# Attention layer of a two-layer backbone: maxima kept in SBUF, query norms cut into pieces with PSUM operands, rotation sums on VectorE, latent keys finished tile by tile

## The chip, the cores and the metric

The program runs on one core of a Trainium2 chip, with one launch for the whole network. The metric is device time in microseconds (us) of that core. Three unprofiled runs of the kernel before took 1298.45, 1296.28 and 1297.53 us (median 1297.53). One further execution was profiled; all durations below come from it.

The core has five engines with an instruction queue each: TensorE (PE in the profile, with its weight loads as PEld), VectorE (DVE), ScalarE (ACT), GpSimd (POOL) and SyncE (SP), which issues most DMA transfers here. Each queue is executed in its order; between queues there are only semaphores. PSUM is the memory that TensorE writes to, in banks of 2 KB per partition; SBUF is the large on-chip memory.

## What is computed

Layer 0 is a bidirectional gated DeltaNet over 512 latent and 256 context tokens; layer 1 is grouped-query attention with an axial rotary embedding; each stands between an adaptive RMS norm and a gated residual, and a last RMS norm ends the network. The change lies in layer 1, but for the helper of the norms, which both layers call. Cut to layer 1, the reference is:

```python
u_lat = rms_norm(h_lat, norm_g[1]) * (1 + scale) + shift          # 512 x 1024
u_ctx = rms_norm(h_ctx, norm_g[1]) * (1 + scale_c) + shift_c      # 256 x 1024
q, k, v, z = split(u @ att_w_in)        # 8 query heads, 2 key/value heads of 128
q = rms_norm(q, q_norm_g); k = rms_norm(k, k_norm_g)              # per head
q_lat, k_lat = axial_rope(q_lat), axial_rope(k_lat)
s = q_lat @ concat(k_ctx, k_lat).T * 128 ** -0.5                  # 512 x 768, each head
y = (softmax(s) @ concat(v_ctx, v_lat) * silu(z)) @ att_w_out
out = rms_norm(h_lat + gate * y, final_norm_g)
```

## The kernel before

All matrices are float32, and every product is made of three matmuls: each operand is split into a rounded part ("hi") and a remainder ("lo"), and hi·hi, hi·lo and lo·hi are summed in PSUM. ScalarE casts the hi part from PSUM, VectorE subtracts it for the lo part; for weights GpSimd does both (`split_w`, L1209 and L1210; for the output weights L1520 and L1521).

**Normed inputs and keys.** Token tiles 0 and 1 hold the context, 2 to 5 the latents. `norms1` (L1160) makes the scale factors of the layer's norm with `rsqrt` (L163), an integer first guess and three Newton steps on VectorE; with the argument `room` its values lie in a transposition tile in PSUM (of these tiles, tag "tr", there are two). `u_block(k)` (L1169) transposes and scales input block k of eight on TensorE into such a tile (ht), VectorE scales it in place (L1176), ScalarE casts it (L1177) and VectorE subtracts (L1178), giving uL. `kv_block` (L1236) adds block k into the key/value accumulators kv2 to kv5: the loop over k runs u_block(k+1), then kv_block(k) for the four latent tiles. So all four tiles are finished together after k = 7. Between them lie the context's key norm (`kv_norm`, after k = 2), its turned keys (`k_turned`, `k_to_T`) and the tables of the rotation (`rope_by`).

**First queries.** After the loop come, written out by hand: the gate projection `z_main(0)`, the norm of all latent keys at once (squares on ScalarE L1248, `rsqrt` with room, then the split of the values L1252 and L1253), and in turn the four query tiles of pair 0 (`q_main`, 24 matmuls each, L1348, into half a bank of pg), with the rotation of a key tile and of a query tile beside each. `rotated` (L1259) makes, for a query, x·cos on VectorE into SBUF (L1264), two products of the swapped halves with sin (L1267), and the sum of the two on GpSimd (L1268); for a key the factor of the norm is in these products (L1271, L1272) and GpSimd adds likewise (L1273). `to_T` then transposes the sum on TensorE (L1279) and splits it (L1281, L1282). `q_post` (L1353) calls the rotation, then has ScalarE sum the squares (qj, L1357); behind the last tile it calls `rsqrt` for the eight norms of the pair, all of it in SBUF (lines L174, L175, L185 and three times L188 to L190). The norm isn't applied to the query but in the softmax, as a scale per row.

**The loop of attention.** For u = 0 to 35 one pass does: `scores(u)` for head u div 4 and query tile u mod 4 (six matmuls L1389 into s3), its maximum (VectorE L1391, into a spare column of po, the PSUM tile of the values), its product with the norm (nm, VectorE L1394), the exponential (pr, ScalarE L1397), reciprocal of the sum (L1398) and scaling (L1403); the transposition of the probabilities of pass u−2 in two halves (`turn`, TensorE L1414, ScalarE L1416, VectorE L1417); in every even pass `values` (18 matmuls L1426 into po, then ay on VectorE L1428, and the split of yT on ScalarE L1430 and GpSimd L1431). A piece of other matmuls is woven in: of every eight passes (a block) the first two and the last two hold halves of a gate projection (`z_main`, L1371), passes 2 to 5 the four query tiles of the next pair (`q_main`); each tile's `q_post` runs one pass later, and its `to_T` a pass after that. From u = 27 the pieces are parts of the output projection (L1445), whose weights are loaded and split from u = 25 on, with two staging buffers (wf, L1518, pool "wo").

(The norm of the context's keys lies in one of the two transposition tiles as well, between two blocks.) From the latents' key stage to the end of this loop the order on TensorE, VectorE and ScalarE is as the code is written (`manual_schedule`); the order on GpSimd and SP follows from a scheduler's own timeline.

## Time and profile before

| | |
|---|---|
| unprofiled runs | 1298.45, 1296.28, 1297.53 us |
| profiled execution: its time | 1297.93 us |
| its span, first to last instruction | 1296.2 us |
| mean granted TensorE clock | 0.966 |
| layer 1, from its first key matmul | 977.4 us after the span's start, so 319 us |

In the profile's rows, times are us from the span's start. A timeline row gives start, duration, engine, line, operation, output tile <- input tiles with partitions x elements, and a count when equal neighbours are merged; brackets hold the idle time of the engine just before it and what ended it. TensorE's idle time starts at the modelled end of the last matmul. A row of groups gives busy time and mean ns. A row of stages gives its bounds, then busy time and count for each engine, and after POOL the granted TensorE clock, 1.00 being full speed.

### The profile page before, as it was taken

To read this page: it belongs to the slowest core of one execution; us is meant where nothing else is said; L and a number is where in the kernel's file an instruction comes from. 1 tells how busy PE (TensorE), PEld (TensorE's weight loads), DVE (VectorE), ACT (ScalarE), POOL (GpSimd) and SP (SyncE) were. 2 spreads that over 40 slices of the span, in tenths; PEclk is the share of its full clock that TensorE was granted. 3 is DMA by queue.
4 is the path that set the end of the run, shared out by engine and by line. 5 is a ranking of instruction groups with operands and counts; after the bars stand their busy time and mean duration, and the time that the engine had idled before them with its cause. 6 is when DMAs were issued, how large, how long until landed. Compare 5 with 4: busy or idle time off the path is not lost.

```text
span 1296.2 us, 28116 instructions
## 1 busy us (share of the span) xinstructions
PE 1170.6 (90%) x10803; PEld 940.9 (73%) x10803; DVE 822.0 (63%) x1800; ACT 705.3 (54%) x1892; POOL 641.8 (50%) x503
## 2 busy tenths in 40 slices
PE   3999999999789898999999988897999787989996
PEld 1676778888678777887666655685787677878874
DVE  2688566777897466765888884754346456555535
ACT  3344336665476768963898874633332244545621
POOL 0121132169989998302665785675662234331540
PEclk9999999999899988999999999998999988989998
DMA  9366976355545597539799666454642021010233
GB/s 315 130 220 206 327 245 169 113 167 167 151 123 184 154 269 239 180 125 283 235 247 246 166 181 172 152 166 134 186 133 66 1 65 50 17 34 33 66 98 97
DMA packets 165351, 204.56 MB, mean 158 GB/s; under 512 B 13377, under 2 KB 114914, under 8 KB 164322
## 3 DMA queue, kind: packets, MB, share of 16 engines
q1 hardware_dynamic: 146402, 193.33, 49.0%
q10 hardware_dynamic: 18816, 9.44, 2.5%
q8 instruction: 85, 1.39, 0.4%
q14 instruction: 48, 0.39, 0.1%
HBM read 161.96 MB, written 40.67 MB: 156 GB/s over the span
## 4 chain that ended last, share of the span: by engine, by line
PE 54%; DVE 14%; POOL 9%; DMA 9%; ACT 8%; issue 4%; SPq 1%; ACTq 0%; DVEq 0%; POOLq 0%
PE ks L979 6%; PE g_q L335 5%; PE po L1138 5%; PE g_v L335 4%; PE g_z L335 4%; PE pg L1348 3%; PE su L1034 3%; PE po L1426 2%; PE g_k L335 2%; PE pg L1371 2%; PE pr L1004 2%; POOL wol L872 2%; POOL X L677 2%; PE pso L1445 2%; POOL tmp L676 2%
## 5 line engine op out<-in xcount | busy, mean ns | idle before, releaser
L987 POOL TENSOR_TENSOR S<-S,glb 128x512 f32<-128x512 f32 x88 | 90.1, 1047 | 112.5 <-PE ks L979 112.4
L1138 PE MATMUL po<-woh,y 128*128 128x512 f32 x384 | 127.8, 403 | 11.1 <-ACT y L900 8.3
L335 PE MATMUL g_v<-uh,wh 128*128 128x512 f32 (+1 forms) x256 | 91.5, 357 | 15.7 <-DVE sil_v L362 15.7
L872 POOL TENSOR_TENSOR wol<-wo,woh 128x1024 fp32r<-128x1024 f32 x32 | 76.3, 2390 | 52.7 <-ACT woh L871 52.4
L677 POOL TENSOR_TENSOR X<-X,tmp 128x62 f32<-128x62 f32 (+15 forms) x93 | 96.8, 1040 | 6.5
L979 PE MATMUL ks<-S,ckq 128*64 128x256 f32 x768 | 93.5, 385 | 3.4 <-ACT o L984 2.7
L357 DVE SCALAR_TENSOR_TENSOR acc_v<-g_v,cwv,acc_v 128x510 f32<-128x510 f32 (+3 forms) x128 | 74.4, 609 | 34.7 <-ACT acc_v L354 33.2
L335 PE MATMUL g_z<-uh,wh 128*128 128x512 f32 (+1 forms) x256 | 88.9, 347 | 4.6 <-DVE sil_v L362 4.5
L676 POOL TENSOR_TENSOR tmp<-L,X 128x62 f32<-128x62 f32 (+15 forms) x93 | 89.1, 958 | 6.9
L1138 PEld LDWEIGHTS po<-woh,y 128*128 128x128 f32 x384 | 71.6, 191 | 27.7 <-ACT y L900 9.2
L335 PE MATMUL g_v<-ul,wh 128*128 128x512 f32 (+1 forms) x256 | 90.0, 352 | 0.0
L335 PE MATMUL g_v<-uh,wl 128*128 128x512 f32 (+1 forms) x256 | 89.2, 349 | 0.0
L335 PE MATMUL g_z<-ul,wh 128*128 128x512 f32 (+1 forms) x256 | 87.4, 342 | 0.0
L335 PE MATMUL g_z<-uh,wl 128*128 128x512 f32 (+1 forms) x256 | 87.3, 341 | 0.0
L979 PEld LDWEIGHTS ks<-S,ckq 128*64 128x64 f32 x768 | 50.7, 136 | 42.6 <-ACT o L984 11.7
L1138 PE MATMUL po<-wol,y 128*128 128x512 f32 x192 | 77.6, 404 | 4.0 <-POOL wol L872 4.0
L317 POOL TENSOR_TENSOR wl_k<-w_k,wh_k 128x1024 fp32r<-128x1024 f32 x8 | 19.0, 2386 | 101.8 <-ACT wh_k L316 101.8
L335 PEld LDWEIGHTS g_v<-uh,wh 128*128 128x128 f32 x256 | 50.8, 198 | 22.5 <-DVE sil_v L362 16.4
L1397 ACT ACTIVATE pr<-s,nm,sq 128x768 f32<-128x768 f32 x32 | 31.8, 993 | 62.9 <-DVE nm L1394 62.4
L1348 PE MATMUL pg<-wq,uL 128*128 128x256 f32 x384 | 56.0, 293 | 5.0 <-ACT qj L1357 2.6
L1052 DVE TENSOR_TENSOR S<-su,S 128x512 f32<-128x512 f32 x88 | 56.5, 683 | 4.1 <-PE su L1034 2.9
L982 DVE SCALAR_TENSOR_TENSOR r<-ks,negV,cv 128x128 f32<-128x128 f32 x192 | 56.1, 343 | 3.3 <-PE ks L979 2.5
(370 smaller groups left out, 3384.6 us busy)
## 6 DMA issues: line engine op xcount, KB each, us to landing
aw<-in_ada_w SPq DMA_DIRECT2D x24, 1024.0 KB, 7.8
w<-in_dn_w_in SPq DMA_DIRECT2D x40, 512.0 KB, 4.4
wo<-in_dn_w_out SPq DMA_DIRECT2D x32, 512.0 KB, 3.3
cv<-v_d SPq DMA_DIRECT2D x80, 128.0 KB, 5.3
df<-gc_d SPq DMA_DIRECT2D x48, 128.0 KB, 2.8
z_d<-zs SPq DMA_DIRECT2D x16, 384.0 KB, 4.9
v_d<-vt ACTq DMA_DIRECT2D x16, 384.0 KB, 3.9
t_d<-Tt SPq DMA_DIRECT2D x6, 1024.0 KB, 4.8
```

Of the source, the lines that this page charges most:

```text
L335: mm = T.matmul(pg_[:m, :n], w[:, k, :m], u[:, k, c0:c0 + n], start=k == 0 and n_ == 0, stop=k == KT - 1 and n_ == 2)
L357: V.scalar_tensor_tensor(acc[:, c0 + lo:c0 + hi], ps[:, lo + j - 2:hi + j - 2], cwv[:, j, ct:ct + 1], acc[:, c0 + lo:c0 + hi], ALU.mult, A ...
L676: E.tensor_tensor(tv, bcast(L[:, :, j + 1:, j], 3, j + 1), bcast(X[:, :, j, 0:j + 1], 2, n), ALU.mult)
L677: E.tensor_tensor(X[:, :, j + 1:, 0:j + 1], X[:, :, j + 1:, 0:j + 1], tv, ALU.subtract)
L872: G.tensor_tensor(wl, w, wh, ALU.subtract)
L979: T.matmul(ks[r0:r0 + 64, w], kq[:, w, slot(hh), r0:r0 + 64], St[hh][:, d], start=True, stop=True)
L982: V.scalar_tensor_tensor(r[:, 2 * j + i], ks[:, 0, i], negV[:, visit, t, h0 + i:h0 + i + 1], v[:, 2 * hh + i], ALU.mult, ALU.add)
L987: G.tensor_tensor(St[hh], St[hh], bcast(g_, 3, P), ALU.mult)
L1034: T.matmul(su[c0:c0 + 64, d ^ j, j], kt[r0:r0 + 64, 4 * j + p, c0:c0 + 64], vd[r0:r0 + 64, 2 * j:2 * j + 2], start=True, stop=True)
L1052: V.tensor_tensor(St[hh], raw(sj, 0, [[512 - 1024 * j, 2], [P, 2], [1, P]]), St[hh], ALU.add)
L1138: T.matmul(acc[j][nh], y[i][:, j, :], ww[k][:, nh * 512:(nh + 1) * 512], start=h == 0 and x == 0, stop=h == VH - 1 and x == 2)
L1348: T.matmul(pgq, uL[i][:, k, t * P:(t + 1) * P], wq[j][:, k], start=k == 0 and n_ == 0, stop=k == KT - 1 and n_ == 2)
```

## The change

It has six parts:

1. The maximum of a row of scores goes to a small SBUF tile (nx) instead of po, and its product with the norm is made by ScalarE (an activation Copy with a scale), in front of the exponential.
2. The norm of a query pair is no longer made in one go in `q_post`. A new generator `q_norm(p)` makes it in four pieces (5, 4, 4 and 4 instructions), with the intermediate values in the free quarter of the transposition tile of `turn`; in the loop a piece follows each VectorE split of `turn` from u = 6 of the block on. For pair 0 the four pieces run in a row before the loop.
3. `rsqrt` with room takes its first steps in PSUM too; it has one instruction more.
4. The sum of a rotation is made by VectorE. The product with cos stays in PSUM: in place for the keys and for pair 0, in the free half of the pg bank for the others. ScalarE's squares of a query tile are issued ahead of its rotation. Of the buffers there are three for the sums (two before) and one for the products with sin (two before).
5. The loop over k for the latent keys covers k = 0 to 3, with two u_blocks ahead of each kv_block; then each tile takes its blocks 4 to 7 by itself. The key norms are made in two pairs of tiles, the values' split (`kv_values`) is a function of its own, and the query tiles of pair 0 are made in the order 0, 2, 1, 3.
6. The staging of the output weights has three buffers.

```diff
 def rsqrt(x, mul=None, add=True, room=None, E=None):
...
-        if not add:
+        if not add or room:
             pass
...
         if room:
             yp, t = room
-            V.tensor_scalar(yp.bitcast(I32), y.bitcast(I32), -1.0, float(0x5F3759DF), ALU.mult, ALU.add)
+            V.tensor_scalar(yp, x, mul, EPS, ALU.mult, ALU.add)
+            V.tensor_copy(x, yp)
+            V.tensor_single_scalar(t.bitcast(I32), yp.bitcast(I32), 1, ALU.logical_shift_right)
+            V.tensor_scalar(yp.bitcast(I32), t.bitcast(I32), -1.0, float(0x5F3759DF), ALU.mult, ALU.add)
...
-    def rotated(x, r, which, t, nm):
+    def rotated(x, r, which, t, nm, room_):
 
-        o = tmp.tile([P, 2, P], F32, tag="qr", name=f"qr{nm}", bufs=2)
-        tm = tmp.tile([P, 2, P], F32, tag="tm", name=f"tm{nm}", bufs=2)
+        o = tmp.tile([P, 2, P], F32, tag="qr", name=f"qr{nm}", bufs=3)
+        tm = tmp.tile([P, 2, P], F32, tag="tm", name=f"tm{nm}", bufs=1)
         if r is None:
-            V.tensor_tensor(o, x, bcast(cg[which][:, t], 1, 2), ALU.mult)
             for s_ in range(2):
                 c, c_ = slice(s_ * 64, s_ * 64 + 64), slice(64 - s_ * 64, 128 - s_ * 64)
                 V.tensor_tensor(tm[:, :, c], x[:, :, c_], bcast(sg[which][:, t, c], 1, 2), ALU.mult)
-            G.tensor_tensor(o, o, tm, ALU.add)
-            return o
...
+            V.tensor_tensor(room_, x, bcast(cg[which][:, t], 1, 2), ALU.mult)
...
-        G.tensor_tensor(o, o, tm, ALU.add)
+        V.tensor_tensor(o, room_, tm, ALU.add)
         return o
...
-    u_block(0, 0, (2, 3, 4, 5), uL)
-    for k in range(KT):
-        if k + 1 < KT:
-            u_block(k + 1, 0, (2, 3, 4, 5), uL)
-        kv_block(k, (2, 3, 4, 5))
-        if k == 2:
-            kv_norm((0, 1), "c")
...
+    LAT = (2, 3, 4, 5)
+    u_block(0, 0, LAT, uL)
+    for k in range(4):
+        for k_ in (2 * k + 1, 2 * k + 2):
+            if k_ < KT:
+                u_block(k_, 0, LAT, uL)
+        kv_block(k, LAT)
+        if k == 1:
+            kv_norm((0, 1), "c")
+            kv_values((0, 1))
+        if k in (2, 3):
+            k_turned(k - 2)
+            rope_by(1, k - 2)
+    for t in LAT:
+        for k in range(4, KT):
+            kv_block(k, (t,))
+        if t < 4:
+            k_to_T(t - 2)
+            rope_by(0, t - 2)
+        if t == 3:
+            kv_norm((2, 3), "a")
+        if t > 3:
+            k_turned(t - 2)
...
     def q_post(p, t):
...
-        qTs["r", p, t] = rotated(pgq.rearrange("p (h d) -> p h d", h=2), None, 0, t, f"q{p}{t}")
+        free = pg[1 - t % 2].rearrange("p (t n) -> p t n", t=2)[:, 1 - t // 2]
+        x, room_ = (y.rearrange("p (h d) -> p h d", h=2) for y in (pgq, pgq if p == 0 else free))
         for h in range(2):
             jk = tmp.tile([P, P], F32, tag="jk", name=f"qj{p}{t}{h}")
             S.activation(jk, pgq[:, h * P:(h + 1) * P], AF.Square, accum_out=sq[:, t, h:h + 1])
-        if t == 3:
-            rsqrt(sq.rearrange("p t h -> p (t h)"), 1.0 / P)
+        qTs["r", p, t] = rotated(x, None, 0, t, f"q{p}{t}", room_)
+
+    def q_norm(p):
+
+        x = qTs["s", p].rearrange("p t h -> p (t h)")
+        y = at.tile([P, 8], F32, tag="qy", name=f"qy{p}", bufs=1)
+        sp = (yield)[:, 0:8]
+        V.tensor_scalar(sp, x, 1.0 / P, EPS, ALU.mult, ALU.add)
+        V.tensor_copy(x, sp)
+        V.tensor_single_scalar(sp.bitcast(I32), sp.bitcast(I32), 1, ALU.logical_shift_right)
+        V.tensor_scalar(sp.bitcast(I32), sp.bitcast(I32), -1.0, float(0x5F3759DF), ALU.mult, ALU.add)
+        V.tensor_copy(y, sp)
+        for i in range(3):
+            sp = (yield)[:, 0:8]
+            V.tensor_scalar(sp, y, -0.5, None, ALU.mult)
+            V.tensor_tensor(sp, sp, y, ALU.mult)
+            V.tensor_tensor(sp, sp, x, ALU.mult)
+            V.scalar_tensor_tensor(x if i == 2 else y, sp, 1.5, y, ALU.add, ALU.mult)
...
-        nm_ = po[:, 256 + 4 * b:257 + 4 * b]
+        nm_ = at.tile([P, 1], F32, tag="nx", name=f"nx{u}", bufs=3)
...
-        V.tensor_tensor(nms, nm_, r, ALU.mult)
+        S.activation(nms, nm_, AF.Copy, scale=r)
...
         S.copy(hi, ps[:, :3])
         V.tensor_tensor(lo, ps[:, :3], hi, ALU.subtract)
+        if chain:
+            try:
+                chain[0].send(ps[:, 3])
+            except StopIteration:
+                chain.pop()
...
+        if u % 8 == 6 and u < 24:
+            chain.append(q_norm(u // 8 + 1))
+            next(chain[0])
...
-                w = wp.tile([P, D], F32, tag="w", name=f"wf{k}")
+                w = wp.tile([P, D], F32, tag="w", name=f"wf{k}", bufs=3)
```

Three places show the order on the engines; a row has the line, the operation, the tile written <- the tiles read, and the shape. The first is VectorE at u = 6 of the first block, behind the last query tile of pair 1 (sq holds the sums of squares, rs and qy are intermediate values, pT the split of a transposed tile pt). Before:

```order
L1267 TENSOR_TENSOR tmq_12754<-pg_12100,sg_11723 128x2x64 x2
L174 TENSOR_SCALAR sq_12494<-sq_12494 128x8
L175 TENSOR_SCALAR rs_19_12763<-sq_12494 128x8
L185 TENSOR_SCALAR rs_19_12763<-rs_19_12763 128x8
...
L190 SCALAR_TENSOR_TENSOR sq_12494<-rs_19_12764,rs_19_12763 128x8
L1391 TENSOR_REDUCE po_12397<-s_12396 128x1
L1394 TENSOR_TENSOR nm_12784<-po_12397,sq_12190 128x1
```

And with the change:

```order
L1277 TENSOR_TENSOR qrq_12791<-pg_12144,tmq_12792 128x256
L1421 TENSOR_REDUCE nx_12804<-s_12424 128x1
L1428 RECIPROCAL sm_12809<-sm_12809 128x1
L1447 TENSOR_TENSOR pT_1_12825<-pt_0_12826,pT_0_12824 128x3x128
L1379 TENSOR_SCALAR pt_0_12826<-sq_12525 128x8
L1380 COPY sq_12525<-pt_0_12826 128x8
L1381 TENSOR_SCALAR pt_0_12826<-pt_0_12826 128x8
L1382 TENSOR_SCALAR pt_0_12826<-pt_0_12826 128x8
L1383 COPY qy_12797<-pt_0_12826 128x8
L1447 TENSOR_TENSOR pT_1_12825<-pt_1_12840,pT_0_12824 128x3x128
```

The twelve steps that stood ahead of the maximum are gone from there; the norm's pieces stand behind the splits of the transposed probabilities, each with an operand in their PSUM tile, and no nm stands on VectorE.

The second place is VectorE in a pass with a rotation, here u = 11, behind the values of passes 6 and 7 (ay). Before:

```order
L1428 SCALAR_TENSOR_TENSOR ay_13083<-po_12397,zt_12466 128x256
L1264 TENSOR_TENSOR qrq_13087<-pg_12101,cg_11721 128x256
L1267 TENSOR_TENSOR tmq_13088<-pg_12101,sg_11723 128x2x64 x2
L1391 TENSOR_REDUCE po_12397<-s_12396 128x1
L1394 TENSOR_TENSOR nm_13104<-po_12397,sq_12494 128x1
L1398 RECIPROCAL sm_13107<-sm_13107 128x1
```

And with the change:

```order
L1465 SCALAR_TENSOR_TENSOR ay_13126<-po_12425,zt_12496 128x256
L1271 TENSOR_TENSOR tmq_13135<-pg_12145,sg_11724 128x2x64 x2
L1272 TENSOR_TENSOR pg_12145<-pg_12145,cg_11722 128x256
L1277 TENSOR_TENSOR qrq_13134<-pg_12145,tmq_13135 128x256
L1421 TENSOR_REDUCE nx_13146<-s_12424 128x1
L1428 RECIPROCAL sm_13151<-sm_13151 128x1
```

One more instruction, the sum qrq, stands ahead of the maximum, and the product with cos (L1272) now writes to PSUM, behind the two others.

The third place is VectorE in the latents' key stage (uL1 the split of a transposed block ht, roomkc the PSUM values of the context's key norm, vv1 the split of its values). Before, with ht3 and three kv_blocks issued on TensorE ahead of it:

```order
L1178 TENSOR_TENSOR uL1_11729<-ht3_0_11924,uL0_11728 128x512
...
L178 TENSOR_SCALAR roomkc_11952<-rs0_16_11953 128x4
...
L183 SCALAR_TENSOR_TENSOR ksq_11753<-roomkc_11952,rs0_16_11953 128x4
L1253 TENSOR_TENSOR vv1_11720<-kv0_11747,vv0_11719 128x256
L1253 TENSOR_TENSOR vv1_11720<-kv1_11748,vv0_11719 128x256
L1176 TENSOR_SCALAR ht4_0_11974<-ht4_0_11974,au1_88 128x512
L1178 TENSOR_TENSOR uL1_11729<-ht4_0_11974,uL0_11728 128x512
L1291 SCALAR_TENSOR_TENSOR kr0_11994<-kv0_11747,ksq_11753,qg_11730 128x128 x2
L1176 TENSOR_SCALAR ht5_0_11999<-ht5_0_11999,au1_88 128x512
```

And with the change, with ht4 and two kv_blocks ahead of it:

```order
L1181 TENSOR_TENSOR uL1_11730<-ht4_0_11922,uL0_11729 128x512
L177 TENSOR_SCALAR roomkc_11950<-ksq_11754 128x4
...
L185 SCALAR_TENSOR_TENSOR ksq_11754<-roomkc_11950,rs0_16_11951 128x4
L1258 TENSOR_TENSOR vv1_11721<-kv0_11748,vv0_11720 128x256
L1258 TENSOR_TENSOR vv1_11721<-kv1_11749,vv0_11720 128x256
L1179 TENSOR_SCALAR ht5_0_11973<-ht5_0_11973,au1_88 128x512
L1181 TENSOR_TENSOR uL1_11730<-ht5_0_11973,uL0_11729 128x512
L1179 TENSOR_SCALAR ht6_0_11981<-ht6_0_11981,au1_88 128x512
L1181 TENSOR_TENSOR uL1_11730<-ht6_0_11981,uL0_11729 128x512
L1295 SCALAR_TENSOR_TENSOR kr0_12001<-kv0_11748,ksq_11754,qg_11731 128x128 x2
```

The norm and the two splits have moved one block later in the order of the blocks and one kv_block earlier in that of TensorE: the next two blocks, ht5 and ht6, stand right behind them, where one had a kv_block between it and the next.

More of the change, by code (lines that the diff above doesn't have):

```diff
@@ L174, in rsqrt @@
             V.tensor_scalar(x, x, mul, EPS, ALU.mult, ALU.add)
-        V.tensor_single_scalar(y.bitcast(I32), x.bitcast(I32), 1, ALU.logical_shift_right)
         if room:
             yp, t = room
-            V.tensor_scalar(yp.bitcast(I32), y.bitcast(I32), -1.0, float(0x5F3759DF), ALU.mult, ALU.add)
+            V.tensor_scalar(yp, x, mul, EPS, ALU.mult, ALU.add)
+            V.tensor_copy(x, yp)
+            V.tensor_single_scalar(t.bitcast(I32), yp.bitcast(I32), 1, ALU.logical_shift_right)
+            V.tensor_scalar(yp.bitcast(I32), t.bitcast(I32), -1.0, float(0x5F3759DF), ALU.mult, ALU.add)
             for i in range(3):
@@ L184, in rsqrt @@
             return
+        V.tensor_single_scalar(y.bitcast(I32), x.bitcast(I32), 1, ALU.logical_shift_right)
         V.tensor_scalar(y.bitcast(I32), y.bitcast(I32), -1.0, float(0x5F3759DF), ALU.mult, ALU.add)
@@ L1250, in kv_norm, with kv_values @@
         rsqrt(kr_, 1.0 / P, room=room(f"k{nm}", 2 * len(tiles)))
+    def kv_values(tiles):
         for t in tiles:
@@ L1267, in rotated @@
                 V.tensor_tensor(tm[:, :, c], x[:, :, c_], bcast(sg[which][:, t, c], 1, 2), ALU.mult)
-            G.tensor_tensor(o, o, tm, ALU.add)
-            return o
-        for h in range(2):
-            V.scalar_tensor_tensor(o[:, h], x[:, h], r[:, h:h + 1], cg[which][:, t], ALU.mult, ALU.mult)
-            V.scalar_tensor_tensor(tm[:, h].rearrange("p (s d) -> p s d", s=2), swapped(x[:, h]), r[:, h:h + 1], sg[which][:, t].rearrange("p (s d) -> p s d", s=2), ALU.mult, ALU.mult)
-        G.tensor_tensor(o, o, tm, ALU.add)
+            V.tensor_tensor(room_, x, bcast(cg[which][:, t], 1, 2), ALU.mult)
+        else:
+            for h in range(2):
+                V.scalar_tensor_tensor(tm[:, h].rearrange("p (s d) -> p s d", s=2), swapped(x[:, h]), r[:, h:h + 1], sg[which][:, t].rearrange("p (s d) -> p s d", s=2), ALU.mult, ALU.mult)
+                V.scalar_tensor_tensor(room_[:, h], x[:, h], r[:, h:h + 1], cg[which][:, t], ALU.mult, ALU.mult)
+        V.tensor_tensor(o, room_, tm, ALU.add)
         return o
@@ L1288, in k_turned @@
         if t < 2:
-            kr = tmp.tile([P, 2, P], F32, tag="qr", name=f"kr{t}", bufs=2)
+            kr = tmp.tile([P, 2, P], F32, tag="qr", name=f"kr{t}", bufs=3)
             for h in range(2):
@@ L1292, in k_turned @@
         else:
-            kr = rotated(x, ksq[:, t], 1, t - 2, f"k{t}")
+            kr = rotated(x, ksq[:, t], 1, t - 2, f"k{t}", x)
         krs[t] = kr
@@ L1417, in turn @@
         V.tensor_tensor(lo, ps[:, :3], hi, ALU.subtract)
+        if chain:
[3 more added lines that the diff above has]
+                chain.pop()
+    chain = []
     def values(u2):
@@ L1456, in backbone @@
     whole(z_main(0, 0))
-    kv_norm((2, 3, 4, 5), "l")
+    kv_values((2, 3))
+    kv_norm((4, 5), "b")
     whole(z_main(0, 1))
-    k_turned(2)
+    k_to_T(2)
+    k_turned(4)
     z_post(0, 1)
     whole(q_main(0, 0))
-    k_to_T(2)
-    k_turned(3)
-    whole(q_main(0, 1))
-    k_to_T(3)
-    q_post(0, 0)
-    k_turned(4)
-    whole(q_main(0, 2))
-    q_to_T(0, 0)
-    k_to_T(4)
-    q_post(0, 1)
-    k_turned(5)
-    whole(q_main(0, 3))
-    q_to_T(0, 1)
+    k_to_T(3)
+    k_turned(5)
+    whole(q_main(0, 2))
+    k_to_T(4)
+    q_post(0, 0)
+    whole(q_main(0, 1))
     k_to_T(5)
     q_post(0, 2)
-    q_post(0, 3)
+    kv_values((4, 5))
+    whole(q_main(0, 3))
+    q_to_T(0, 0)
+    q_post(0, 1)
+    q_to_T(0, 2)
+    q_post(0, 3)
+    g_ = q_norm(0)
+    next(g_)
+    sp = ptr.tile([P, 4, P], F32, tag="tr", name="roomq0")[:, 3]
+    for _ in range(4):
+        try:
+            g_.send(sp)
+        except StopIteration:
+            pass
     psG_c.__exit__(None, None, None)
@@ L1482, in backbone @@
     po = pS.tile([P, 512], F32, tag="po", name="po1")
-    posts, turns = {}, {0: (0, 2), 1: (0, 3)}
+    posts, turns = {}, {0: (0, 1), 1: (0, 3)}
     for u in range(32 + 4):
```

7 lines of the change are left out of this document (removed).

## The prediction

> **What bounds the kernel now.** I read the page first, then who TensorE waits for inside layer 1, then those places on the timeline, then the granted clock in short stages around them.
>
> ```profile
> span 1296.2 us, 28116 instructions
> PE 54%; DVE 14%; POOL 9%; DMA 9%; ACT 8%; issue 4%; SPq 1%; ACTq 0%; DVEq 0%; POOLq 0%
> ```
>
> The chain that ended last is over half TensorE. Layer 0's instructions are not touched, so the time can only move in the last 319 us. There, TensorE's own waits (us in total, times, longest) are:
>
> ```profile
> PE po L1426 <- DVE nm L1394: 14.2, 4, 5.7
> PE s L1389 <- ACT pr L1397: 6.6, 2, 6.2
> PE qtq L1279 <- DVE pT L1417: 2.9, 3, 1.0
> PE qtq L1279 <- POOL qrq L1268: 2.7, 1, 2.7
> PE pg L1445 <- POOL wo L1521: 2.6, 2, 2.1
> PE pg L1348 <- ACT qj L1357: 2.6, 1, 2.6
> PE pg L1348 <- DVE qrk L1271: 2.4, 1, 2.4
> PE kv L1240 <- ACT uL L1177: 0.9, 2, 0.6
> ```
>
> They come to 34.9 us in 16 stops; between them TensorE runs without a gap, so layer 1 is bound by TensorE and by these chains behind it. A stop also slows what follows:
>
> ```profile
> 1028.10 4.51 PE L1348 MATMUL pg<-wq,uL 128*128 128x256 f32 x24 [2.63 <-ACT qj L1357]
> 1085.42 4.09 PE L1426 MATMUL po<-pT,vv 128*128 128x256 f32 x18 [5.65 <-DVE nm L1394]
> ```
>
> ```profile
> 1024.42:1027.83 3.41, 1.05 (x10) 0.81 (x8) 2.14 (x8) 1.17 (x5) 0.49 (x1) 1.00 0.00 0
> 1027.83:1031.24 3.41, 3.14 (x14) 3.15 (x15) 0.38 (x2) 0.21 (x2) 0.97 (x2) 0.50 0.01 2
> 1031.24:1034.66 3.42, 1.81 (x15) 1.57 (x14) 1.39 (x5) 0.65 (x2) 1.98 (x2) 1.00 0.00 0
> 1034.66:1038.07 3.41, 2.37 (x13) 2.05 (x14) 2.62 (x6) 1.61 (x9) 3.19 (x4) 1.00 0.00 0
> 1044.90:1048.31 3.41, 1.94 (x6) 1.66 (x7) 0.79 (x4) 2.27 (x4) 1.04 (x1) 0.50 0.35 90
> 1048.31:1051.72 3.41, 3.41 (x10) 2.73 (x10) 1.29 (x3) 1.55 (x3) 0.00 (x0) 0.50 0.18 63
> 1085.86:1089.27 3.41, 3.41 (x18) 3.41 (x18) 1.19 (x3) 2.18 (x5) 0.00 (x0) 0.50 0.00 0
> 1140.47:1143.88 3.41, 3.41 (x17) 3.41 (x17) 1.19 (x3) 2.33 (x5) 0.00 (x0) 0.50 0.01 4
> 1232.63:1236.04 3.41, 1.32 (x8) 0.87 (x6) 1.55 (x3) 1.49 (x3) 3.41 (x3) 1.00 0.00 0
> 1236.04:1239.46 3.42, 3.42 (x12) 2.83 (x12) 0.17 (x1) 0.36 (x1) 3.05 (x3) 0.50 0.50 153
> ```
>
> The second figure is TensorE's busy time, the third from the end the granted clock. Stages of 3.41 us on one fixed grid show either 1.00 or 0.50. Busy for 1.05 or 1.32 us (31 and 39%), a stage is followed by one at half clock; busy for 1.81 (53%), it is not. Half the busy time of a stage at 0.50 is what the clock cost: 1.7 us in a full one.
>
> **The change part by part.** The sum is made against the profiled execution, 1297.93 us (span 1296.2 plus 1.7 around it).
>
> *A, maxima and norms in the loop.* Values wait for nm because the maximum lies in their PSUM tile po; and the norm stands ahead of that maximum, long because of these two steps:
>
> ```profile
> 1077.81 2.30 DVE L175 TENSOR_SCALAR rs<-sq 128x8 int32<-128x8 int32 x1
> 1080.15 2.26 DVE L185 TENSOR_SCALAR rs<-rs 128x8 int32<-128x8 int32 x1
> ...
> 1077.71 4.67 POOL L1210 TENSOR_TENSOR wq<-w1q,wq 128x1024 fp32r<-128x1024 f32 x2
> ...
> 1108.13 0.16 DVE L1394 TENSOR_TENSOR nm<-po,sq 128x1 f32<-128x1 f32 x1
> ...
> 1106.54 2.39 POOL L1210 TENSOR_TENSOR wz<-w1z,wz 128x1024 fp32r<-128x1024 f32 x1
> ```
>
> Each ends with one of GpSimd's two splits, while nm, which has an operand in PSUM, takes 0.16 inside such a split. So I take the new steps, all with a PSUM operand, as unheld at 0.2 each, 17 to a block: 3.4 us in four pieces. Removed are 14.2 us of idle time, the 0.16 that each stop costs beyond its column (my reading of starts against the modelled ends), so 0.6, and two full stages at half clock, 3.4: 18.2. Left: the piece of five steps (1.0) delays the second split of the probabilities, for which the second half of the values (nine of 18 matmuls, about 1.1 at the full clock) is cover only in part, and the next exponential; I take 0.7 in each of three blocks. A is **−16.2** (bounds −18.2, and −12 if each block lost 2). The product on ScalarE costs about 0.2 in place of 0.16 on VectorE; the nearest row:
>
> ```profile
> L521 ACT COPY rq<-ss_q 128x6 f32<-128x6 f32 x8 | 1.3, 163 | 1.3 <-PE ss_q L491 1.3
> ```
>
> It lies on the same chain, maximum to exponential, and ScalarE is only half busy there; 32 times ±0.1 is hidden but for the last passes.
>
> *B, first queries and first scores.* The three stops of 2.4, 2.6 and 2.7 and the one of 6.2 (6.6 with a later one) go: 14.3, with 0.6 for the starts, and the clock cost 3.14/2 + 1.94/2 + 3.41/2 = 4.2; together 19.1. What is late next is the sum of tile 1: behind the last projection TensorE has only two short transpositions, while ScalarE squares (0.63) and VectorE makes two products, product, sum and a split (0.48, 0.41, 0.41, 0.42) and an earlier split: a stop of about 2.8. Then scores(1) wait for the first exponential: tile 3's rotation 1.3, norm 3.4, maximum 0.96, nm 0.2, exponential 1.0 (993 ns on the page, L1397), 6.9 in all, against 1.3 of scores and 3.1 of gate matmuls (at half clock for a while): about 1.8, and 0.5 in the next two. With one stage at half clock (1.7) 6.8 stays. B is **−12.3** (bounds −9 and −15).
>
> *C, staging.* The two stops of 2.6 are waits for GpSimd, which itself waits for transfers into two buffers; a third lets each start one split (2.38) earlier. Idle 2.6 and 0.3, clock 1.7, less 0.4 left: **−4.2** (bounds 0, −4.6).
>
> *D, the sum on VectorE.* This adds to the chain ahead of the maximum:
>
> ```profile
> 1112.53 0.41 DVE L1264 TENSOR_TENSOR qrq<-pg,cg 128x256 f32<-128x256 f32 x1
> 1112.86 0.48 DVE L1267 TENSOR_TENSOR tmq<-pg,sg 128x128 f32<-128x128 f32 x2
> 1113.26 0.96 DVE L1391 TENSOR_REDUCE po<-s 128x1 f32<-128x768 f32 x1
> ...
> 1112.65 0.41 ACT L1430 CAST yT<-ay 128x256 fp32r<-128x256 f32 x1 [1.60 <-DVE ay L1428]
> 1113.43 0.28 ACT L1357 ACTIVATE qj<-pg 128x128 f32<-128x128 f32 x1 [0.38 <-DVE tmq L1267]
> 1113.70 0.27 ACT L1357 ACTIVATE qj<-pg 128x128 f32<-128x128 f32 x1
> ```
>
> Squares now come first and VectorE's products wait for them. Here the cast ends at 1113.06, squares 0.6 later at 1113.65, then 0.48, 0.41 and 0.41 less overlaps of 0.1: the maximum starts near 1114.85, not 1113.26, 1.6 later. In the odd passes, which have no values, the transpositions' splits queue behind this pass's exponential, and TensorE ends its 24 matmuls and waits: for tile 2's pass that is the 2.9 in three stops, for tile 0's just no stop. Tile 0's grow by 1.6; in tile 2's the rotation already waited for a cast, and growth is the sum and the uncovered part of the squares, about 0.8. Six stops of 1.6 to 1.8, about 10.2 in place of 2.9, and 0.5 for three more starts: +7.8. In the six even passes the values (2.3 us) hide it; if that cover is gone, each costs what the chain has over it. Stops of 1.8 leave a stage 47% busy, between the 39% and the 53% above; I take one half-clock stage, +1.7. D is **+9.5** (bounds +7 and +18). Price of a PSUM result, the same operation with each (SBUF first):
>
> ```profile
> L298 DVE TENSOR_SCALAR u<-px,au 128x512 f32<-128x512 f32 x8 | 6.5, 809 | 1.8 <-PE px L296 1.3
> ...
> L1176 DVE TENSOR_SCALAR ht<-ht,au 128x512 f32<-128x512 f32 x8 | 6.5, 814 | 5.0 <-PE ht L1174 5.0
> ```
>
> 5 ns, so the in-place product is taken at 0.41, as before.
>
> *E, latent keys.*
>
> ```profile
> 975.94 0.82 DVE L1176 TENSOR_SCALAR ht<-ht,au 128x512 f32<-128x512 f32 x1 [1.91 <-PE ht L1174]
> 977.47 0.69 DVE L1178 TENSOR_TENSOR uL<-ht,uL 128x512 fp32r<-128x512 f32 x1 [0.71 <-DMA w1z<-in_att_w_in]
> ...
> 988.85 3.05 PE L1240 MATMUL kv<-wkv,uL 128*128 128x512 f32 x12
> ...
> 990.78 0.16 DVE L183 SCALAR_TENSOR_TENSOR ksq<-roomkc,rs 128x4 f32<-128x4 f32 x1
> ```
>
> A block's transposition tile is free 2.2 us after VectorE starts on it, and there are two tiles. Blocks two ahead make the third wait with one block's matmuls (0.8) as cover: 1.5. Of the pair behind the second kv_block, the first waits about 1.0 for block 3's split; the second's tile is the one in which the context's norm is made, which ended at 990.9 and can hardly end earlier, its VectorE work ahead being the same, while TensorE comes there one kv_block (3.05) earlier, less 0.4: 2.6. Idle 5.1 against 0.9 (and as much again in small ones) and 0.5 for starts: +3.8. The stage from 986.87 on that same grid is then busy for about 1 us, so its successor falls, and some 5 us of keys cost 2.5 more. E is **+6.3**, all later work hidden (bounds +1 and +8). What it buys, keys ready earlier, is in B.
>
> *F.* In the last passes the exponentials (ScalarE) come 0.2 later each, about +1.0; two more steps in the norm of the latents, on the path to the first key: +0.4. **+1.4**.
>
> Sum: −16.2 − 12.3 − 4.2 + 9.5 + 6.3 + 1.4 = −15.5, so 1282.4 against 1297.93, and 1282.0 against the median of 1297.53.
>
> **A rule of the skill about the clock.** The row at 1232.63 falls after stops of at most 2.1 us (the longest of its line above). The Trainium skill (TensorE: Matmul & The Clock Gate, section "HAM oscillation — how this bites in real kernels") puts the fall at TensorE gaps of more than about 3.4 us; by it none of the stops that I leave would slow the clock, and the sum would be that of the second case below.
>
> **The rivals.**
> 1. *The forecast*, 1278 to 1286: 0.60.
> 2. *The clock doesn't fall* at the stops left: less 1.7 (B), 1.7 (D) and 2.5 (E), so 1276. The stops left are at most 2.8 us and can straddle two stages of the grid; against it speak the stages of 31 and 39%. 0.13.
> 3. *VectorE's four instructions of a rotation are somewhat dearer in their new form* (product in place in PSUM, sum from PSUM and SBUF), by 0.1 each: six odd passes 2.4, first queries and keys 1.2, and stops of 2.2 that now lower the clock, two or three times 1.7: 1288 to 1291. Nothing in the profile shows a product in place with a dependent one behind it. 0.13.
> 4. *The norms aren't freed*: steps that read or write an SBUF operand are still held to the end of a split. That is the change not doing what it says. Two of three blocks meet two splits (4.6 us of holding), with about 2.3 behind the values as cover: 2 × 2.3, 1287. The row of nm at 1108.13 speaks against it, though its shape is 128x1. 0.06.
> 5. *Slower than before*: the same four instructions cost 0.25 us more each, because each waits for the one ahead to be written out to PSUM. Then odd passes lose 6.0, the even ones outgrow their cover of some 0.6 and lose 6 × 0.4 = 2.4, queries and keys 3.0, and stops of 2.8 lower the clock about five more times, 8.5: 19.9, so 1302. It decides from about 0.2 each (4.8 + 1.2 + 2.4 + 6.8 = 15.2). The 5 ns above speak against it. 0.05.
>
> The remaining 0.03 is for mixtures that end within 0.2% (about what a measurement of this kernel can tell from no change). So faster 0.92, same 0.03, slower 0.05. The range goes from 1275 (case 2, and a shorter D) to 1291 (case 3 in full); it leaves out case 5, the mixtures and the edges of the others, under 2 in 10.
>
> **What would show it.** In the profile after: values without a wait for nm or its successor; the norm's steps near 0.2 beside GpSimd's splits (case 4 if any is near 2.3); six stops of about 1.8 at the turned query tiles in odd passes and none above 0.6 in even ones (cases 3 and 5 otherwise); a stop near 2.6 at about 990 with a half-clock stage behind it (case 2 if the clock stays); one stop near 2.8 behind the last projection of pair 0; the sum's instruction near 0.41. The forecast is wrong if a transfer or GpSimd, which has 20 instructions less, becomes the one waited for, or if the stops of D are absent.

## The result and the profile after

| | kernel before | changed kernel |
|---|---|---|
| median of 5 runs each | 1298.39 us | 1276.45 us (1274.45 to 1281.36) |
| ratio | 1 | 0.9843, 95% interval 0.9817 to 0.9869 |
| profiled execution | 1297.93 us | 1275.92 us |
| start of layer 1 (first transposition of the latents) | 974.85 us | 972.32 us |
| from there to the end of the span | 321.3 us | 301.8 us |

The kernel is 1.6% faster, and its time lies near the low end of the range given, 1275 to 1291. The profiled execution gained 22.0 us where the sum said 15.5. Of this, 19.5 us lie behind the first transposition of the latents and 2.5 us ahead of it. Nearly all of these 2.5 belong to the change too: part 3 reaches the norm of the context's inputs, which is made while layer 0's last products still run. Its first two steps on VectorE, GpSimd's additions beside them, and TensorE's next matmul, before:

```profile
878.86 1.19 DVE L174 TENSOR_SCALAR hrc<-hrc 128x2 f32<-128x2 f32 x1
880.08 1.19 DVE L175 TENSOR_SCALAR rs<-hrc 128x2 int32<-128x2 int32 x1
878.75 2.50 POOL L1144 TENSOR_TENSOR h<-h,gy 128x512 f32<-128x512 f32 x2
883.78 0.80 PE L1138 MATMUL po<-woh,y 128*128 128x512 f32 x1 [6.95 <-ACT y L900]
```

And with the change, where both steps have an operand in PSUM:

```profile
878.48 0.16 DVE L177 TENSOR_SCALAR roomhc<-hrc 128x2 f32<-128x2 f32 x1
878.68 0.16 DVE L178 COPY hrc<-roomhc 128x2 f32<-128x2 f32 x1
878.39 2.48 POOL L1147 TENSOR_TENSOR h<-h,gy 128x512 f32<-128x512 f32 x2
881.03 0.79 PE L1141 MATMUL po<-woh,y 128*128 128x512 f32 x1 [4.58 <-ACT y L903]
```

The operand that TensorE waits for there (y) is made on VectorE and ScalarE, behind this norm in VectorE's queue. The stop is 6.9 us in all four profiles without part 3 (6.94 to 6.95) and 4.6 in all nine with it (4.56 to 4.59), 2.4 us less. The rest of layer 0 differs from execution to execution: layer 1 began between 968.5 and 977.3 us in those profiled for this study. Layer 1 is therefore measured from its own start below.

The page after the change:

```profile
span 1274.1 us, 28118 instructions
PE 46%; DVE 16%; ACT 13%; POOL 9%; DMA 9%; issue 5%; SPq 1%; ACTq 0%; DVEq 0%; POOLq 0%
```

TensorE's share of the last chain has fallen from 54 to 46%, ScalarE's has risen from 8 to 13. Most of TensorE's fall lies in layer 0's part of the chain (from 501 to 419 us); in layer 1 it went from 198 to 169 us, and ScalarE from 26 to 56: more of the exponentials, their nm and the squares are now on it. Whom TensorE waits for in layer 1 (us in total, times, longest):

```profile
PE qtq L1283 <- DVE pT L1447: 10.6, 6, 2.0
PE s L1419 <- ACT pr L1427: 3.5, 4, 1.9
PE qtq L1283 <- DVE qT L1286: 2.6, 1, 2.6
PE ht L1177 <- DVE uL L1181: 2.2, 2, 1.5
PE ht L1177 <- DVE ksq L185: 2.2, 1, 2.2
PE po L1463 <- ACT pT L1446: 0.7, 1, 0.7
```

The waits of the values on nm (14.2 us) are gone, and so are those on GpSimd. The row that stood for 2.9 us in three stops is now 10.6 us in six: the turned query tiles of odd passes. The two rows of ht are the new stops among the latents' keys. At the place where the norm of pair 1 held everything for 5.65 us, TensorE's timeline is now without a gap:

```profile
1071.99 2.31 PE L1463 MATMUL po<-pT,vv 128*128 128x256 f32 x18
1074.35 0.41 PE L1283 MATMUL qtq<-ident,qrq 128*128 128x128 f32 x2
1074.51 1.28 PE L1419 MATMUL s<-kT,qT 128*128 128x512 f32 x6
```

### The profile page after: what moved, and what is told of

Same layout as the page of the kernel before. It is cut to its first block, busy times and chain, and to the rows that moved or that the text cites. A ratio compares the mean times of both kernels' runs of the same rounds, so it can differ in the third digit from the quotient of the medians.

```text
span 1274.1 us, 28118 instructions
## 1 busy us (share of the span) xinstructions
PE 1164.8 (91%) x10803; PEld 935.6 (73%) x10803; DVE 820.4 (64%) x1828; ACT 711.5 (56%) x1924; POOL 627.2 (49%) x483
## 4 chain that ended last, share of the span: by engine, by line
PE 46%; DVE 16%; ACT 13%; POOL 9%; DMA 9%; issue 5%; SPq 1%; ACTq 0%; DVEq 0%; POOLq 0%
PE ks L982 6%; PE po L1141 4%; PE g_q L338 4%; PE su L1037 3%; PE g_k L338 2%; PE kv L1243 2%; POOL X L680 2%; POOL wol L875 2%; PE g_z L338 2%; PE pg L1361 2%; PE po L1463 2%; PE pr L1007 2%; POOL tmp L679 2%; DVE acc_v L360 2%; PE pso L1482 2%
## 5 line engine op out<-in xcount | busy, mean ns | idle before, releaser
L982 PEld LDWEIGHTS ks<-S,ckq 128*64 128x64 f32 x768 | 51.3, 138 | 42.8 <-ACT o L987 11.0
L1468 POOL TENSOR_TENSOR yT<-ay,yT 128x256 fp32r<-128x256 f32 x16 | 11.8, 736 | 99.3 <-ACT yT L1467 99.3
L338 PEld LDWEIGHTS g_z<-uh,wh 128*128 128x128 f32 x256 | 48.9, 191 | 10.3 <-DVE sil_v L365 5.2
```

Source lines behind the costliest of these rows:

```text
L338: mm = T.matmul(pg_[:m, :n], w[:, k, :m], u[:, k, c0:c0 + n], start=k == 0 and n_ == 0, stop=k == KT - 1 and n_ == 2)
L982: T.matmul(ks[r0:r0 + 64, w], kq[:, w, slot(hh), r0:r0 + 64], St[hh][:, d], start=True, stop=True)
```

## The experiments

Every run is compared in layer 1, by its profile (one execution each), since layer 0 differs from execution to execution; the ratio is to runs of the kernel before on the same chip. The runs maxima_only, norms_only and norms_and_staging lack part 3, and so also its 2.4 us ahead of layer 1. "Key stage" is the stretch from the first transposition of the latents to the first gate matmul, "first stage" from there to scores(3).

| run | time, us | ratio to before (interval) | layer 1 | key stage | first stage |
|---|---|---|---|---|---|
| kernel before | 1298.39 | 1 | 321.3 | 32.7 | 49.8 |
| changed kernel | 1276.45 | 0.9843 (0.9817 to 0.9869) | 301.8 | 35.4 | 37.6 |
| maxima_only | 1297.22 | 0.999 (0.9968 to 1.0011) | 321.2 | 32.7 | 51.2 |
| norms_only | 1273.57 | 0.9815 (0.9793 to 0.9837) | 298.0 | 32.7 | 44.7 |
| norms_and_staging | 1274.35 | 0.9819 (0.9793 to 0.9845) | 294.3 | 32.7 | 42.8 |
| norm_in_sbuf | 1282.59 | 0.9884 (0.9864 to 0.9905) | 308.6 | 38.1 | 41.5 |
| sum_gp_first | 1267.77 | 0.9779 (0.9756 to 0.9803) | 294.2 | 35.4 | 37.5 |
| sum_v_behind | 1269.39 | 0.9783 (0.976 to 0.9807) | 296.2 | 36.8 | 37.5 |
| sum_gp_behind | 1266.64 | 0.9758 (0.9738 to 0.9778) | 292.9 | 38.1 | 37.5 |
| keys_by_block | 1277.56 | 0.9842 (0.9814 to 0.9869) | 302.4 | 33.0 | 40.5 |
| sum_gp_old_keys | 1267.61 | 0.9753 (0.9725 to 0.978) | 292.3 | 33.0 | 42.0 |
| all_but_sum | 1268.07 | 0.9767 (0.9746 to 0.9788) | 293.4 | 37.3 | 37.5 |
| keys_norm_later | 1262.92 | 0.9724 (0.9697 to 0.9751) | 288.1 | 32.9 | 38.0 |

### Which part carries the gain: maxima or norms

maxima_only is the kernel before with part 1:

```diff
-        nm_ = po[:, 256 + 4 * b:257 + 4 * b]
+        nm_ = at.tile([P, 1], F32, tag="nx", name=f"nx{u}", bufs=3)
...
-        V.tensor_tensor(nms, nm_, r, ALU.mult)
+        S.activation(nms, nm_, AF.Copy, scale=r)
```

> The kernel before with part 1 alone: maximum in SBUF, product with the norm on ScalarE; the norms stay in one go ahead of the maximum, with SBUF operands. The values no longer wait for nm, but nm and the exponential are as late as before, so the same 4.6 us turn up a little later, at the scores or the transpositions that need this exponential: layer 1 within 3 us of 321.3. If the shared tile was the cause, the stops of 5.7 go and layer 1 is 8 to 14 us shorter.

Layer 1 took 321.2 us, as before. The stop moved: TensorE's timeline at the end of the first block, and its waits in layer 1, were

```profile
1083.73 2.31 PE L1426 MATMUL po<-pT,vv 128*128 128x256 f32 x18
1091.79 0.66 PE L1279 MATMUL qtq<-ident,qrq 128*128 128x128 f32 x2 [5.75 <-DVE pT L1417]
```

```profile
PE qtq L1279 <- DVE pT L1417: 16.1, 6, 5.8
PE s L1389 <- ACT pr L1397: 7.3, 3, 6.2
```

The values run on (2.31 us, no gap), and the very next transposition waits 5.75 us, for a split that stands on VectorE behind the same norm. The shared PSUM tile was where the wait showed, not what it was for. (Only the fourth of these stops, 1.4 us at u = 26, is the tile's: it is gone here, with the norm as it was.)

norms_only is the kernel before with part 2 (`q_norm` and its calls as in the change; maximum, nm, rotations and keys untouched).

> The kernel before with part 2 alone: the query norms in pieces with PSUM operands; the maximum stays in po and nm on VectorE, rotations and keys as before. If the norm's place ahead of the maximum and its held steps are the whole of the four waits of the values (14.2 us and two stages at half clock) and of the wait of 6.2 us before scores(1), then layer 1 (321.3 us from the first transposition of the latents to the end of the span) loses 16 us in the loop and 4 to 6 at the first scores, about 299 to 302, though nm is still in po. If the shared PSUM tile counts by itself, stops of values on nm remain and it is 305 or more.

Layer 1 took 298.0 us, 23.3 less and 3.8 less than with the whole change. From scores(3) to scores(31) it lost 16.2 us and in the first stage 5.1, as the first theory had it; the 2.0 behind scores(31) that take it below 299 were not expected. Its remaining waits of TensorE, without the first stage's:

```profile
PE qtq L1279 <- DVE pT L1432: 3.5, 4, 1.0
...
PE pg L1467 <- POOL wo L1554: 1.9, 3, 0.9
PE po L1448 <- DVE nm L1409: 1.4, 1, 1.4
```

So the norms alone carry more than the net gain, with the maxima where they were; of the waits on nm only the one at u = 26 stays, which isn't at a norm.

### What the PSUM operand does

norm_in_sbuf is the changed kernel with the same pieces at the same places, but in an SBUF tile:

```diff
-        sp = (yield)[:, 0:8]
+        sb = at.tile([P, 8], F32, tag="qz", name=f"qz{p}", bufs=1)
+        yield
+        sp = sb
...
-            sp = (yield)[:, 0:8]
+            yield
```

> The changed kernel with the pieces of the norm in an SBUF tile instead of the free quarter of the transposition tile; same pieces, same places. If the PSUM operand is what frees the steps from GpSimd's splits, some of the 17 steps of blocks 1 and 2 last up to 2.3 us again, and layer 1 is 3 to 9 us longer than 301.8. If the place alone did it (the splits end before the pieces come), all steps stay near 0.17 and layer 1 within 1 us.

Layer 1 took 308.6 us, 6.8 more. 2.7 of these are half clock among the keys (38.1 against 35.4), which has nothing to do with the norm; 4.0 lie in the first stage, where TensorE waited 4.4 us for the first exponential (and one more stage was at half clock); in the loop passes 6 to 9, 14 to 17 and 22 to 24, behind the pieces, cost 2.3, and passes 3 and 4, without the changed kernel's half-clock stage, gave 2.2 back. One step of the norm in the last pass of block 0, in the changed kernel (VectorE, GpSimd) and then in this run (same order):

```profile
1080.50 0.17 DVE L1387 TENSOR_TENSOR pt<-pt,qy 128x8 f32<-128x8 f32 x1
...
1080.41 2.39 POOL L1213 TENSOR_TENSOR wz<-w1z,wz 128x1024 fp32r<-128x1024 f32 x1
```

```profile
1084.65 2.41 DVE L1389 TENSOR_TENSOR qz<-qz,qy 128x8 f32<-128x8 f32 x1
...
1084.64 2.40 POOL L1213 TENSOR_TENSOR wz<-w1z,wz 128x1024 fp32r<-128x1024 f32 x1
```

Both start beside a split. With an operand in PSUM the step takes 0.17 us, with two in SBUF it ends with the split. So both matter: the place (only four of the 68 steps of the four norms were held) and the operand.

### The rotation: sum and squares

Three runs change `rotated` and `q_post` for pairs 1 to 3 only, in the changed kernel: sum_gp_first puts the sum back on GpSimd, with the product in SBUF; sum_v_behind puts ScalarE's squares behind the rotation again; sum_gp_behind does both.

```diff
-            V.tensor_tensor(room_, x, bcast(cg[which][:, t], 1, 2), ALU.mult)
+            V.tensor_tensor(o if room_ is None else room_, x, bcast(cg[which][:, t], 1, 2), ALU.mult)
+            if room_ is None:
+                G.tensor_tensor(o, o, tm, ALU.add)
+                return o
...
```

> The rotations of pairs 1 to 3 go back to what they were: product with cos in SBUF, sum on GpSimd, squares behind the rotation. If the six stops of 1.7 to 2.0 us in odd passes (10.9 us in the changed kernel) come from the longer chain ahead of the maximum, they shrink to three stops of about 1 us, and layer 1 is 8 to 10 us shorter than in the changed kernel (301.8 us from the first transposition of the latents to the end of the span), so about 1266 to 1268 in time. Rival: the stops come from the product with the norm on ScalarE (the exponential now starts 0.27 us later); then stops of about 1.5 stay and the gain is under 3 us.

> The sum stays on VectorE, only the squares of pairs 1 to 3 go behind the rotation. If the order of the squares is the larger part of the growth (0.6 us of squares ahead of the products), tile 0's three stops fall by about 0.9 and tile 2's by about 0.2 to 0.5, and layer 1 is 4 to 6 us shorter than in the changed kernel. If the sum itself is the whole of it, it stays within 1 us of the changed kernel.

> The sum on GpSimd, the squares ahead of the rotation. If the sum and the squares simply add in the chain, this takes 0.34 us from each of the six odd passes plus what dependent products cost (0.1), so layer 1 is 3 to 6 us shorter than in the changed kernel, and the gains of this run and of the one with squares behind add up to that of both together within 2 us. If one covers the other, this one alone brings nearly all or nearly nothing.

Layer 1 took 292.9, 296.2 and 294.2 us: 8.9, 5.6 and 7.6 us less than the changed kernel. These totals don't add up, since half clock among the keys (2.7, 1.4 and 0 us more than in the changed kernel), the stage at half clock at 1052 that all three lack and another order of the last matmuls (1.4, below) are in each; the stops do. TensorE's waits on the splits of the transposed probabilities, in the order sum_gp_behind, sum_v_behind, sum_gp_first:

```profile
PE qtq L1286 <- DVE pT L1456: 3.7, 4, 1.0
```

```profile
PE qtq L1283 <- DVE pT L1452: 7.0, 6, 1.6
```

```profile
PE qtq L1286 <- DVE pT L1451: 5.1, 4, 1.5
...
PE qtq L1286 <- POOL wq L1212: 2.5, 2, 1.2
```

10.6 us become 7.0 with the squares behind, 7.6 with the sum away (the trace puts two of these stops on GpSimd), and 3.7 with both. That is 3.6, 3.0 and 6.9: they add up within 0.3. With the squares behind, tile 0's stops fell by 0.8, 1.1 and 1.1 and tile 2's by 0.2 each, near the 0.9 and the 0.2 to 0.5 expected. The rival of the first run, nm on ScalarE, is out: it stayed there in all three, and it delays an exponential by 0.07 us, not 0.27 (the exponential starts 0.36 us after the end of the maximum, 0.29 before the change). sum_gp_first gained more than the 6 us expected at most, by that stage and that order. For pair 0 and the keys the sum stays on VectorE in all three. That it pays there is likely, but not shown: the first stage took 44.7 and 42.8 us in the two runs with the old rotation (norms_only, norms_and_staging), 40.5 with the new one and the old loop over the keys (keys_by_block), but that run also makes the query tiles in the new order and the key norms in pairs.

### Latent keys

keys_by_block brings the old loop back into the changed kernel, sum_gp_old_keys into sum_gp_behind:

```diff
-    for k in range(4):
-        for k_ in (2 * k + 1, 2 * k + 2):
-            if k_ < KT:
-                u_block(k_, 0, LAT, uL)
+    for k in range(KT):
+        if k + 1 < KT:
+            u_block(k + 1, 0, LAT, uL)
         kv_block(k, LAT)
...
-    for t in LAT:
-        for k in range(4, KT):
-            kv_block(k, (t,))
...
+    kv_norm((2, 3), "a")
+    k_turned(2)
+    k_turned(3)
```

> The loop over the latents' keys goes back to one block ahead and all four tiles finished together, with the norm and rotation of tiles 2 and 3 behind the loop; the rest is the changed kernel. By the terms of the prediction the stops of 1.5, 0.7 and 2.2 us go (4.4, against 1.4 to 1.8 before) but the keys are ready later, and the stages with the first queries wait for them: from the first transposition of the latents to the first gate matmul 32.7 us instead of 35.4, and about as much later lost, so layer 1 within 3 us of the changed kernel. If the part pays as it stands, layer 1 is 3 us longer or more; if it only costs, 3 us shorter.

> The run with the sum on GpSimd and squares behind, with the old loop over the latents' keys. Keys by tile cost as much ahead of the first gate matmul as they give behind it, so layer 1 is within 1.5 us of that run at full clock (290.1, that is 292.9 less the 2.7 of its half-clock stage); and as its key stage has no stop over 0.7 us, no stage at half clock falls there.

keys_by_block took 302.4 us in layer 1, 0.6 more than the changed kernel: 2.3 us less in the key stage, 2.9 more in the first stage, where the key tiles' norm is waited for. sum_gp_old_keys took 292.3 against 290.1 for sum_gp_behind at full clock, 2.2 more and so past the 1.5 expected; but a stage at half clock fell at another place, at 1018.6 us, behind that same wait. TensorE was busy throughout it (3.41 us), so it cost about 1.7, and like for like 0.5 us are left. Keys by tile, as written, are worth nothing measurable.

all_but_sum and keys_norm_later try to mend the key stage of sum_gp_behind. The first makes the context's key norm without a transposition tile and takes one block less ahead; the second leaves both and moves the norm one turn later:

```diff
-        if k == 1:
+        if k == 2:
             kv_norm((0, 1), "c")
             kv_values((0, 1))
-        if k in (2, 3):
-            k_turned(k - 2)
-            rope_by(1, k - 2)
     for t in LAT:
         for k in range(4, KT):
             kv_block(k, (t,))
...
+        if t == 2:
+            k_turned(0)
+            k_turned(1)
+            rope_by(1, 0)
...
```

> The changed kernel with the rotations of pairs 1 to 3 as they were (as in the run with sum on GpSimd and squares behind), the context's key norm in SBUF instead of a transposition tile, and one input block less ahead in the first turn of the key loop. Against the run with the sum on GpSimd (292.9 us in layer 1, with the key stage partly at half clock) the stops of 2.2 and 1.5 us at the keys go and with them the cause of the half clock there: 286 to 290 in layer 1, about 1260 to 1264 in time. If the stop of 2.2 isn't due to the tile of the norm, it stays, and only 1 to 2 us are gained.

> The run with the sum on GpSimd and squares behind, with the context's key norm moved one turn later in the key loop (behind the third kv_block instead of the second, the tiles' turning behind it). If the stops of 0.7 and 2.2 us at the keys come from VectorE's queue, in which the norm stands ahead of the split that the second of two blocks waits for, both go, the stage no longer loses its clock, and the time from the first transposition of the latents to the first gate matmul falls from 35.4 (at full clock; 38.1 with the half-clock stage) to 32 to 33 us; layer 1 about 287 us, the time about 1262. If it is only the transposition tile that the norm occupies, a stop of about 2 us turns up at the last input block instead and it stays near 35.

all_but_sum missed: 293.4 us (1.4 of them another order of the last matmuls, below). On its timeline the stops had mostly moved, with 3.1 us in the key stage where there had been 4.4:

```profile
993.77 1.13 PE L1177 MATMUL ht<-dn,h 128*128 128x128 f32 x8 [1.50 <-DVE uL L1181]
995.84 2.05 PE L1177 MATMUL ht<-dn,h 128*128 128x128 f32 x8 [0.94 <-DVE uL L1181]
```

The norm no longer sat in a tile, the key stage was again in part at half clock (37.3), and the pair of blocks behind it still waited, for the split of a block that VectorE had queued behind norm and values. In keys_norm_later the norm kept its tile and the stops of 0.7 and 2.2 shrank to one of 0.7: key stage 32.9 us, layer 1 288.1 us, both as expected.

These two runs don't decide between tile and queue as the expectations meant. The last input block was to show a stop of about 2 us if it were the tile; but in keys_norm_later its transposition runs ahead of the norm's first step:

```profile
991.13 1.13 PE L1177 MATMUL ht<-dn,h 128*128 128x128 f32 x8 [0.66 <-DVE uL L1181]
991.34 0.17 DVE L177 TENSOR_SCALAR roomkc<-ksq 128x4 f32<-128x4 f32 x1 [0.35 <-ACT kj L1251]
```

So it lies in the other of the two tiles, and the run takes the block out of the way of both. What is shown: in the changed kernel the stop of 2.2 us ends with the norm's last step, which frees the tile (the row of ht and ksq above); and without the tile, in all_but_sum, VectorE's queue alone still made stops of 1.5 and 0.9 us. Moving the norm by a turn cures both. At 0.9724 of the time before, this version is faster than both kernels of the comparison.

### Staging

> The kernel before with parts 2 and 6 alone: norms in pieces, three staging buffers (paid for with a single buffer for the products with sin). Against the run with part 2 alone (298.0 us in layer 1) the three waits for the output weights (1.9 us) go, so 296 to 297; the single buffer may add a wait of about 1 us where tile 2 and tile 3 of pair 0 are turned back to back. If the maxima's place (part 1) is needed besides, the stop of 1.4 us of the values at u = 26 stays as it was.

norms_and_staging (wf with bufs=3 and tm with bufs=1 in norms_only) took 294.3 us in layer 1, 3.7 less than norms_only, though its median time is the same within the interval. No wait on the output weights is left, which is 1.5 us behind scores(31). 1.9 us of the 3.7 are the first stage, which had three stages at half clock in the profile of norms_only and one here, though a stop of 1.3 us was added. The stop at u = 26 stayed at 1.4.

## Why the prediction came out as it did

**The sign, and the sum of the terms in the loop, held.** Where TensorE's passes start gives each term. *A*: from scores(6) to scores(7) before took 1075.03 to 1089.49 = 14.46 us, and after 1067.40 to 1074.51 = 7.11; with the three other places (7.30, 1.46, 1.07) and 1.02 given back behind the pieces, −16.2, as the sum had it. *B*: the first stage went from 49.75 to 37.55, −12.2, for −12.3. *D*: scores(3) to scores(6) is 4.4 us longer, and 2.5 in each of blocks 1 and 2, +9.4, for +9.5. The forecast of six stops of 1.6 to 1.8 (one is 2.0) with one half-clock stage among them, at 1052, came out, and the 2×2 of runs shows that squares and sum made them, in about the shares that the step gave. The even passes hid the chain. *C* and the tail together are −3.1 (−3.46 behind scores(31), +0.32 ahead of it), forecast −3.2.

Two of these agreements are in part luck. The 1.02 is not the pieces' doing: sum_gp_behind has the same pieces and the old rotation, and its passes 7 and 8 take 4.57 and 6.62 us, as before the change (4.58 and 6.63), and pass 6 takes 6.84, not 7.11. By cause *A* is about −18, *D* about +10 (the changed kernel against sum_gp_behind from scores(3) to scores(31): 168.7 and 158.4 us), and the 0.7 that *A* allowed for in each block didn't come. And of the 3.5 us behind scores(31), norms_only, with two staging buffers, already had 2.0; the third buffer brought 1.5, where *C* gave it 4.2.

**The waits, and the reason given under A.** The eight rows of the prediction hold 34.9 us; all of TensorE's waits in layer 1 before were 35.8 us in 19 stops, so it didn't run quite without a gap between them. The reason under A was half wrong. The step put the values' wait on the shared tile po and on the norm. maxima_only gained nothing on balance; the norm was all of it but the 1.4 us at u = 26. The number was right because the two were never priced apart.

**What was mis-sized is E and the start.** E was forecast at +6.3 and measured +2.7 (35.37 − 32.70). Its idle time was near: 1.5, 0.7 and 2.2, so 4.4 for 5.1. The 2.5 us at half clock didn't come, and the reason is where the stops fell on the clock's grid. The changed kernel at the keys, then sum_gp_behind, which has the same code and stops there:

```profile
983.69:987.10 3.41, 2.00 (x12) 1.34 (x10) 2.17 (x11) 2.16 (x11) 0.00 (x0) 1.00 0.02 8
987.10:990.51 3.41, 1.92 (x12) 1.75 (x13) 2.59 (x11) 0.55 (x1) 0.00 (x0) 1.00 0.00 0
```

```profile
983.35:986.76 3.41, 1.38 (x10) 0.97 (x8) 2.57 (x13) 1.69 (x11) 0.00 (x0) 1.00 0.01 2
986.76:990.17 3.41, 2.52 (x10) 2.43 (x11) 2.62 (x9) 0.59 (x1) 0.00 (x0) 0.51 0.00 0
990.17:993.59 3.42, 3.42 (x9) 2.65 (x9) 2.75 (x7) 0.59 (x1) 0.00 (x0) 0.50 0.00 0
```

In the one the stops of 0.7 and 2.2 us straddle two stages, which stay busy for 2.00 and 1.92 us; in the other one stage holds most of them, 1.38 us are left, and the next two run at half clock. The key stage is 38.1 us there, 2.7 more: the price was right, but whether it is paid is not settled by the code: of the five profiles with this code at the keys, two took 35.4 us, one 36.8 and two 38.1. So the profile's 1275.92 is a run without it. E's cause was right as far as it went: the step named the tile of the norm, on which the stop does end; that VectorE's queue stands behind it, all_but_sum showed.

The start is the step that failed outright. The prediction held that layer 0's instructions were not touched, so that time could only move in the last 319 us, and gave part 3 only a cost, +0.4 for the norm of the latents. That cost was 0.1 (from this norm's first instruction to the first transposition 8.0 us, 7.9 before), and the same part took 2.4 us off a stop ahead of layer 1. So the time lies in the range, but below the forecast's own 1278 to 1286, by two things that the sum didn't have: no half clock at the keys, and the freed norm of the context.

**The rivals.** That the clock doesn't fall at all gave 1276 and would have fitted the time. It held at the keys, where stops straddled two stages as that case had it, but not elsewhere. The clock did fall twice, behind the first and the third of these rows, and not behind the last:

```profile
1024.65:1028.06 3.41, 1.45 (x13) 1.22 (x11) 2.72 (x9) 1.16 (x6) 2.27 (x3) 1.00 0.00 0
1028.06:1031.47 3.41, 2.81 (x9) 2.44 (x10) 2.75 (x13) 1.00 (x5) 3.41 (x2) 0.51 0.03 9
...
1048.54:1051.95 3.41, 1.52 (x14) 1.32 (x12) 1.73 (x5) 2.29 (x6) 0.00 (x0) 1.00 0.22 76
1051.95:1055.37 3.42, 3.32 (x13) 3.04 (x14) 2.53 (x8) 1.57 (x6) 0.00 (x0) 0.51 0.00 0
...
1164.59:1168.01 3.42, 1.65 (x14) 1.44 (x14) 1.74 (x4) 2.78 (x6) 0.00 (x0) 1.00 0.32 107
```

The stops there are of 2.6 and 2.0 us. The Trainium skill (TensorE: Matmul & The Clock Gate, section "HAM oscillation — how this bites in real kernels") would have asked for more than about 3.4; the trace does not agree. Dearer rotation instructions (cases 3 and 5) did not show: the product in place took 0.43 where 0.41 was taken, the sum 0.42. Held norms (case 4) did not show either, and norm_in_sbuf shows what they would have cost, some 4 us on balance.

## What to carry over

A wait names the place where an engine stopped, not what to change: taking one operand out of the shared tile moved a stop of 5.7 us to the next transposition, taking the long run of steps off VectorE's queue removed it. Work moved onto the engine in front of a maximum or an exponential is paid for in every pass that has no other matmuls to hide it, here 10 us in the loop for 12 sums and the order of 24 squares. A helper that several places call changes all of them: look for its callers ahead of the stretch that the change is about. Where a clock depends on a grid of stages, price a stop by what it costs alone and say that the rest comes and goes.
